# A mixer block's opening in written order: query tiles in two pairs, context statistics and first spectrum between the blocks of the first value head

## The chip, the cores and the metric

The kernel runs on one core of a Trainium2 chip. The metric is the device time of one launch in microseconds, the median of the runs shown; smaller is better. A core has five engines, each with its own queue of instructions: TensorE (PE, matrix products), VectorE (DVE), ScalarE (ACT), GpSimd (POOL, here mostly stores) and SyncE (SP, here all loads). An engine waits for another, or for a transfer, on semaphores.

## The reference

One layer of a backbone: two token mixers beside each other on the same normalised input (an mLSTM and a Hyena long convolution), a gated merge, and a feed-forward part. 512 latent tokens and 256 context tokens have 1024 features. What the opening computes of it:

```python
silu_c = jax.nn.silu(c);  silu_cc = jax.nn.silu(c_ctx)
mod  = silu_c  @ w_ada + b_ada          # shift sh1, scale sc1, ...
modc = silu_cc @ w_ada + b_ada
hc = rmsnorm(ctx, norm1_g) * (1.0 + csc1) + csh1
h  = rmsnorm(x,   norm1_g) * (1.0 + sc1)  + sh1
q  = h @ w_in[:, query columns] + b_in
vh = h (and hc) @ w_in[:, value columns] + b_in
g  = h (and hc) @ w_in[:, 16 gate columns] + b_in
# Hyena filters, for two orders and 1024 channels
a = sin(fr * (z @ w1 + b1)); a = sin(fr * (a @ w2 + b2)); a = sin(fr * (a @ w3 + b3))
k = (a @ w4) * window;  spectrum = rfft(two-sided k)
```

## The kernel before

Activations lie feature by feature: eight tiles of 128 features by 512 latent tokens, and eight of 128 by 256 context tokens. Every large product is made of three: each operand is split into a high part (rounded to the matrix format, `act.activation` with Copy) and a low part (the rest, `dve.tensor_sub`), and high by high, high by low and low by high are added in one PSUM bank (`mm3`, lines 233 to 235; in `v_head` lines 659 to 661).

The opening, in the order of the program's text:

- **Loads** (lines 261 to 1087, all on SyncE's queue): a table of vectors, the gate bias, the filter network's weights (`net`), the input `xT` in four pieces, constant matrices, the first half of the adaLN weights (sixteen pieces of 256 KB, `ada_load`) with the first query weights among them, then the first spectrum's decay row, skip and weights, three query weights, the Fourier table, the second adaLN half, and the context `cxT`. Each query weight is 512 KB, each of the four pieces of `xT` as well; `net` has 386 KB, the vectors 190, the constants 320, the gate bias 8, decay 256, skip 1, spectrum weights 256, the Fourier table 640, the context 1024.
- **Statistics** of the latent tokens: squares on ScalarE, sums on VectorE (`sq_sums`, lines 395 to 406), a product with ones, the reciprocal root (`rms_bcast`: scaling on VectorE at line 389, a power on GpSimd at line 391, a broadcast product at line 393), and the multiplication of the tiles (L1063, L1124).
- **adaLN** (`ada_first`, called for each half of the features): 32 products with the silu of both conditions in 32 rows (L337), a copy (L343), two transposes (L346), the additions of the bias (L353) and the scale vector (L354).
- **The filter network** (`filter_network`): three layers, each one product (L419, L422), six operations for the argument of the sine on VectorE (L425 to L430) and a sine on ScalarE (L432), then a split `stack`.
- **Modulation and the first four query tiles**: `modulate` makes high and low parts of the modulated tiles (L1094, L1099, L1100). `part(i, p)` adds for query tile i the products of feature half p. Half 0 needs the first adaLN half, half 1 the second.
- **The first spectrum** (`filter_spectrum`): eight products with the stack (L463, L464), then Fourier products (L233 to L235 on `dfh`, `dfl`).
- **Context**: statistics and eight tiles (L1150 the multiplication; `modulate` with `on_act`, where ScalarE makes both the high part, L1094, and the full value, L1097, and VectorE subtracts, L1100).
- **Value head 0** (`v_head`): six token blocks of 24 products, four latent and two of the context; each is followed by the bias on VectorE (L665), a store on GpSimd (L669) and the gate columns (L671). Then heads 1 to 3 with three larger blocks each, the other spectra between them, and the rest of the layer.

The order on each engine is not that of the text: a scheduler places instructions by their dependencies and priorities, and the text steers it in some places with `tc.issue_after(...)`, which lets what is inside come only after a given instruction, and with `tc.high_priority`. Loads wait for the buffers that they fill.

## Time and profile before

| | |
|---|---|
| median of 3 runs | 1218.85 us (1218.58 to 1222.32) |
| the profiled execution | 1219.83 us |
| its span, first to last instruction | 1218.0 us |
| TensorE busy | 1180.8 us, 97% |
| VectorE busy | 833.2 us, 68% |
| ScalarE busy | 528.9 us, 43% |
| GpSimd busy | 87.7 us, 7% |
| mean granted TensorE clock | 0.992 |

All views are of the one profiled execution, with times from the start of its span. A row of the timeline has the start in us, the duration in us, the engine, the line, the operation, the tile written and those read, the shape, the count of instructions merged into the row and, in brackets, how long the engine had sat idle before it and what ended that. PEclk is the share of full clock that TensorE was granted. `x4` on a row means four records; a product in plain float32 leaves two.

### The profile page before, as it was taken

The numbers are of one execution on the slowest core, as the hardware profiler recorded it, in microseconds if no ns is written. First come the engines' busy times: TensorE is split into PE (matmuls) and PEld (weight loads), VectorE is DVE, ScalarE is ACT, GpSimd is POOL, SyncE is SP. The second block draws the span as 40 slices with busy tenths as digits, with TensorE's granted clock in tenths as the row PEclk, the third lists the DMA queues.
The fourth block names the chain that finished last, engine by engine and source line by source line (L and its number), as shares of the span: only waits on it lengthen the run. The fifth ranks groups of instructions, "written<-read, shape, count | busy, mean of one in ns | idle before, by whom it ended". The sixth has DMA issues, their size and how long they took to land.

```text
span 1218.0 us, 16831 instructions
## 1 busy us (share of the span) xinstructions
PE 1180.8 (97%) x6440; PEld 1012.9 (83%) x6440; DVE 833.2 (68%) x1336; ACT 528.9 (43%) x824; POOL 87.7 (7%) x168
## 2 busy tenths in 40 slices
PE   4999999999999999999989999999999999999997
PEld 2799988888888888888778988889888888888886
DVE  5967797978989999897758896767753434432332
ACT  3754465753545444453655642333432232322221
POOL 0011110100010010101032031000000000000000
PEclk9999999999999999999989999999999999999998
DMA  9744453364244353434695686773443333233312
GB/s 346 248 159 163 136 185 106 133 237 143 75 162 137 130 174 102 147 106 155 211 319 180 196 265 218 260 234 121 140 138 104 90 100 101 85 95 96 96 48 70
DMA packets 63377, 189.04 MB, mean 155 GB/s; under 512 B 8760, under 2 KB 12608, under 8 KB 61120
## 3 DMA queue, kind: packets, MB, share of 16 engines
q1 hardware_dynamic: 51536, 150.20, 38.6%
q0 software_dynamic: 11760, 37.76, 8.7%
q8 instruction: 51, 0.84, 0.3%
q14 instruction: 30, 0.25, 0.1%
HBM read 154.37 MB, written 33.55 MB: 154 GB/s over the span
## 4 chain that ended last, share of the span: by engine, by line
PE 89%; DVE 4%; DMA 3%; ACT 2%; issue 1%; POOL 0%; SPq 0%; DVEq 0%; POOLq 0%; ACTq 0%
PE bank L233 26%; PE bank L234 26%; PE bank L235 26%; PE bank L659 2%; PE bank L660 2%; PE bank L661 2%; DMA wr<-qd 1%; DMA wr<-in_wph 1%; PE bank L616 1%; PE bank L463 1%; DVE wl L215 1%; PE bank L464 1%; ACT wh L214 1%; DMA ul<-in_xT 1%; PE bank L337 0%
## 5 line engine op out<-in xcount | busy, mean ns | idle before, releaser
L233 PE MATMUL bank<-hTh,wh 128*128 128x512 f32 (+1 forms) x952 | 366.6, 387 | 2.9 <-ACT hTh L1094 2.0
L234 PE MATMUL bank<-hTl,wh 128*128 128x512 f32 (+1 forms) x952 | 366.1, 386 | 2.9 <-DVE hTl L1100 2.2
L235 PE MATMUL bank<-hTh,wl 128*128 128x512 f32 (+1 forms) x952 | 365.6, 385 | 0.0
L214 ACT ACTIVATE wh<-wr 128x1024 fp32r<-128x1024 f32 (+1 forms) x167 | 172.2, 1033 | 400.8 <-PE bank L234 205.1
L215 DVE TENSOR_TENSOR wl<-wr,wh 128x1024 fp32r<-128x1024 f32 (+1 forms) x167 | 197.8, 1187 | 170.9 <-ACT wh L214 169.6
L233 PEld LDWEIGHTS bank<-hTh,wh 128*128 128x128 f32 x952 | 178.9, 188 | 37.5 <-ACT hTh L1094 2.2
L234 PEld LDWEIGHTS bank<-hTl,wh 128*128 128x128 f32 x952 | 179.0, 188 | 36.8 <-DVE hTl L1100 2.5
L235 PEld LDWEIGHTS bank<-hTh,wl 128*128 128x128 f32 x952 | 179.0, 188 | 34.6
L233 PE MATMUL bank<-big,wh 128*128 128x512 f32 (+1 forms) x266 | 94.7, 356 | 0.0
L234 PE MATMUL bank<-big,wh 128*128 128x512 f32 (+1 forms) x266 | 94.6, 356 | 0.0
L235 PE MATMUL bank<-big,wl 128*128 128x512 f32 (+1 forms) x266 | 94.6, 355 | 0.0
L372 DVE SCALAR_TENSOR_TENSOR wr<-wr,crow 128x1024 f32<-128x1024 f32 x32 | 38.9, 1218 | 28.3 <-DMA wr<-in_wada 28.2
L233 PEld LDWEIGHTS bank<-big,wh 128*128 128x128 f32 x266 | 50.3, 189 | 7.2
L235 PEld LDWEIGHTS bank<-big,wl 128*128 128x128 f32 x266 | 50.3, 189 | 7.1
L234 PEld LDWEIGHTS bank<-big,wh 128*128 128x128 f32 x266 | 50.3, 189 | 7.1
L214 ACT ACTIVATE hb<-hb 128x512 fp32r<-128x512 f32 (+1 forms) x49 | 36.5, 767 | 33.3 <-DVE hb L468 18.5
L1554 DVE TENSOR_TENSOR s<-s,bank 128x512 f32<-128x512 f32 x22 | 15.1, 686 | 46.4 <-PE bank L235 46.4
L391 POOL TENSOR_TENSOR rr<-rv,negh 128x2 f32<-128x2 f32 (+1 forms) x6 | 5.5, 924 | 510.7 <-DVE rv L389 510.7
L215 DVE TENSOR_TENSOR hb<-hb,hb 128x512 fp32r<-128x512 f32 (+1 forms) x49 | 40.4, 858 | 2.0 <-ACT hb L214 1.8
L659 PE MATMUL bank<-wh,hTh 128*128 128x256 f32 (+1 forms) x128 | 36.4, 285 | 0.0
L661 PE MATMUL bank<-wh,hTl 128*128 128x256 f32 (+1 forms) x128 | 36.4, 285 | 0.0
L660 PE MATMUL bank<-wl,hTh 128*128 128x256 f32 (+1 forms) x128 | 36.4, 284 | 0.0
(383 smaller groups left out, 2208.2 us busy)
## 6 DMA issues: line engine op xcount, KB each, us to landing
wr<-in_win SPq DMA_DIRECT2D x64, 512.0 KB, 3.8
wr<-in_w SPq DMA_DIRECT2D x60, 512.0 KB, 3.5
wr<-in_wada SPq DMA_DIRECT2D x32, 512.0 KB, 4.1
Kd<-K POOLq DMA_DIRECT2D x8, 1024.0 KB, 4.7
K<-Kd SPq DMA_DIRECT2D x8, 1024.0 KB, 6.4
wr<-in_wv SPq DMA_DIRECT2D x8, 512.0 KB
gmd<-s POOLq DMA_DIRECT2D x16, 256.0 KB, 2.5
wr<-in_wph SPq DMA_DIRECT2D x8, 512.0 KB, 4.2
```

The lines of the kernel that those rows point to most:

```text
L214: act.activation(hi, x, AF.Copy)
L215: dve.tensor_sub(lo, x, hi.bitcast(F32))
L233: pe.matmul(o, wh, xh, start=first, stop=False)
L234: pe.matmul(o, wh, xl, start=False, stop=False)
L235: return pe.matmul(o, wl, xh, start=False, stop=last)
L372: dve.scalar_tensor_tensor(w, w, 1.0, crow[:], op0=ALU.mult, op1=ALU.mult, accum_out=s)
L463: pe.matmul(ps[:], lhs, w4h, start=True, stop=False)
L464: pe.matmul(ps[:], lhs, w4l, start=False, stop=True)
L659: pe.matmul(o, xh, wh, start=bool(k == 0), stop=False)
L660: pe.matmul(o, xh, wl, start=False, stop=False)
L661: m = pe.matmul(o, xl, wh, start=False, stop=bool(k == KT - 1))
L1554: dve.tensor_tensor(t[:], t[:], pb[:], op=ALU.mult)
```

## The change

The opening is written as two blocks under a new context manager `in_order`, which makes every instruction of an engine depend on the one before it in the text. So inside, each engine runs what the text says, in the text's order. What the text now says:

- `xT` is loaded first, then vectors and constants, the first adaLN half, four query weights, `net`, the second adaLN half, the context, and last the first spectrum's tables. The gate bias comes with the value weights.
- The query weights are split in halves of four features (`early_hi`, `early_lo`), two of the first modulated tiles get their high part on VectorE (`hi_dve`), and `early_q` adds products by kind: for each tile first the high parts with both weights, later the low parts. Pieces of the second adaLN half and the first two layers of the filter network stand between them.
- The second half of the features is done for query tiles 0 and 1, then 2 and 3.
- `v_head` now yields after the products and after the bias of each block. Between the blocks of head 0 stand the end of the context statistics, the third network layer, the context tiles one after the other, the stack, the first spectrum's products, and the Fourier table's split.
- Behind that, head 1 may start on VectorE and ScalarE only after the fifth context tile (`marked`).

```diff
+    @contextmanager
+    def in_order():
+        traced = nc.cur_bb.bb.instructions
+        n, last, ends = len(traced), {}, []
+        yield ends
+        for i in traced[n:]:
+            if i.engine in last:
+                tc.add_manual_dep(
+                    i, last[i.engine], mybir.DependencyInfo(mybir.DependencyClass.NoSync, mybir.DependencyReason.DATA), reason="in_order"
+                )
+            last[i.engine] = i.name
+        ends.extend(i for i in traced[n:] if i.name in last.values())
...
+    def modulate(x, hi, lo, k, i, hi_dve=False, on_act=False):
+        a_, b_ = amod[:, k, i : i + 1], modT[:, 0, k, i : i + 1]
+        if hi_dve:
+            dve.tensor_scalar(hi, x, a_, b_, op0=ALU.mult, op1=ALU.add)
+        else:
+            act.activation(hi, x, AF.Identity, bias=b_, scale=a_)
+        yield
+        if on_act:
+            t = x
+            act.activation(t, x, AF.Identity, bias=b_, scale=a_)
...
+        dve.tensor_sub(lo, t, hi.bitcast(F32))
+        yield
...
+    def early_q(i, ks, w, x):
+        for k in ks:
+            count[i] += 1
+            m = pe.matmul(qps[i][:], early[i][w][:, k], hT[x][k][:], start=count[i] == 1, stop=count[i] == 3 * KT)
...
+    with in_order() as ends:
+        for q in range(4):
+            t = T(PH, [128, 2, SEQ], F32, ("uh", "ul")[q % 2])
+            dma(t[:], I["xT"][:, 2 * q : 2 * q + 2])
...
+            if q == 2:
+                dma(vecs[:], I["vecs"])
+        dma(mats[:], I["mats"])
...
+        units = [ada_load(PH, 0, slots[0])]
+        for i in range(NQ):
+            dma(raws[i], I["win"][FT_Q + i])
+        dma(net[:, :772], I["net"])
+        units.append(ada_load(PH, 1, slots[1]))
...
+        early_q(1, KA, 0, 1)
+        ahead(4)
+        early_q(2, KA, 0, 1)
+        early_q(3, KA, 0, 1)
...
-    with tc.issue_after(high), tc.issue_after(low):
-        part(0, 1)
-        csums, cb_ = bank(), bank()
-        for k in range(KT):
-            sq_sums(ac_, cxt[k], k, 2, PH, "s2", csums)
-        next(sp0)
-        part(1, 1)
-        rms_bcast(csums[:, :2], 2, cb_, PH, "s2")
-        part(2, 1)
-        for k in range(KT):
-            dve.tensor_tensor(cxt[k], cxt[k], cb_[:, :CTX], op=ALU.mult)
-        part(3, 1)
-        list(sp0)
...
-    for k in range(KT):
-        modulate(cxt[k], hcT[0][k], hcT[1][k], k, 1, True)
...
+    with in_order():
...
+        next(v0)
+        sq_sums(ac_, cxt[KT - 1], KT - 1, 2, PH, "s2", csums)
+        next(network)
+        next(v0)
+        next(v0)
+        rms_bcast(csums[:, :2], 2, cb_, PH, "s2")
+        for k in range(KT):
+            dve.tensor_tensor(cxt[k], cxt[k], cb_[:, :CTX], op=ALU.mult)
+            for _ in modulate(cxt[k], hcT[0][k], hcT[1][k], k, 1, on_act=True):
+                pass
+            if k == 4:
+                marked = list(nc.cur_bb.bb.instructions)
+                next(v0)
+                next(v0)
+        next(v0)
+        next(v0)
         stack = next(network)
+        next(v0)
         act.activation(dec[:], dec[:], AF.Abs)
         w4s = T(PH, [128, 2, 512], F32R, "hb")
         split(w4s[:, 0], w4s[:, 1], w4r)
...
+        open_spectrum = [spectrum(*sp.pop(0), (dec, skip, (w4s[:, 0], w4s[:, 1])))]
+        next(v0)
+        next(open_spectrum[0])
         split(fh[:], fl[:], fr)
...
+        list(v0)
+        next(open_spectrum[0])
+    opened.close()
+    for e in {i.engine for i in marked if i.engine in (nc.vector.engine, nc.scalar.engine)}:
+        opened.enter_context(tc.issue_after([i for i in marked if i.engine == e][-1]))
```

Three places show how the rows stand on the engines (the written order of the built program; a number behind a name is that of a buffer).

The first is SyncE's queue from the last pieces of the first adaLN half (into `K`) to the first piece of the second (into `hTh`). Before (`fd` is the decay row, `hb` the spectrum's weights and the Fourier table, `wr` the query weights):

```order
L325 DMA wr_144<-in_win 128x1024
L328 DMA K_157<-in_wada 128x512 x4
L448 DMA fd_293<-in_hdec 128x512
L450 DMA fs_295<-in_hskip 1x256
L1081 DMA hb_143<-in_hw 128x512
L1083 DMA wr_145<-in_win 128x1024
L1083 DMA wr_146<-in_win 128x1024
L1083 DMA wr_147<-in_win 128x1024
L1084 DMA hb_143<-in_dftf 128x1280
L328 DMA hTh_158<-in_wada 128x512
```

Now (`hb` from `in_net` is the filter network):

```order
L339 DMA K_129<-in_wada 128x512 x4
L339 DMA K_130<-in_wada 128x512 x4
L1108 DMA wr_117<-in_win 128x1024
L1108 DMA wr_118<-in_win 128x1024
L1108 DMA wr_119<-in_win 128x1024
L1108 DMA wr_120<-in_win 128x1024
L1109 DMA hb_103<-in_net 128x772
L339 DMA hTh_131<-in_wada 128x512
```

The spectrum's loads have moved behind the second adaLN half; the query weights and `net` stand ahead of it.

The second is VectorE at the end of the context statistics: `rv` is the scaling ahead of the power on GpSimd. Before, with the split of the value weights around it:

```order
L403 TENSOR_TENSOR s_39_133<-s_39_133,s_149_553 128x256
L215 TENSOR_TENSOR wl_697<-wr_695,wh_696 128x1088
L389 TENSOR_SCALAR rv_577<-bank_532 128x2
L215 TENSOR_TENSOR wl_704<-wr_702,wh_703 128x1088
L215 TENSOR_TENSOR wl_892<-wr_890,wh_891 128x512
L1150 TENSOR_TENSOR K_318<-K_318,bank_533 128x256
```

Now, where `hb_347` is the argument of the third network layer's sine and `bank_571` holds value block 0:

```order
L414 TENSOR_TENSOR s_69_193<-s_69_193,s_149_596 128x256
L436 TENSOR_SCALAR hb_347<-bank_602,hb_103 128x512
L437 TENSOR_SCALAR hb_347<-hb_347 128x512
L438 TENSOR_SCALAR hb_347<-hb_347 128x512
L439 SCALAR_TENSOR_TENSOR hb_347<-hb_347 128x512
L440 SCALAR_TENSOR_TENSOR hb_347<-hb_347 128x512
L441 TENSOR_SCALAR hb_347<-hb_347 128x512
L679 TENSOR_TENSOR s_151_611<-bank_571,s_131_506 128x256
L685 TENSOR_TENSOR gates_85<-bank_571,bgb_86 128x16
L400 TENSOR_SCALAR rv_640<-bank_522 128x2
```

The network layer and the block's two additions have come in front of the scaling. On TensorE there now stand, from the end of block 0 (`bank_571`) over block 1 (`bank_615`) to the start of block 2:

```order
L674 MATMUL bank_571<-wh_516,hTl_458 128x272
L417 MATMUL bank_522<-mats_70,s_69_193 128x1 x2
L433 MATMUL bank_602<-hb_347,hb_103 128x256 x2
L672 MATMUL bank_615<-wh_509,hTh_291 128x272
...
L674 MATMUL bank_615<-wh_516,hTl_458 128x272
L404 MATMUL bank_523<-mats_70,rr_642 128x128 x2
L672 MATMUL bank_670<-wh_509,hTh_291 128x272
```

The sums (L417) and the third layer (L433) follow block 0, and the broadcast (L404) follows block 1.

The third is VectorE and ScalarE in the context tiles (`K` is the context, `hb` its high and low parts). Before, on VectorE:

```order
L1150 TENSOR_TENSOR K_318<-K_318,bank_533 128x256
L215 TENSOR_TENSOR wl_929<-wr_927,wh_928 128x1024
L1150 TENSOR_TENSOR K_318<-K_318,bank_533 128x256 x7
L502 TENSOR_TENSOR hb_657<-bank_617,hb_657 128x512
L1100 TENSOR_TENSOR hb_668<-K_318,hb_667 128x256
L503 TENSOR_TENSOR hb_657<-bank_617,hb_657 128x512
L1100 TENSOR_TENSOR hb_668<-K_318,hb_667 128x256
```

And on ScalarE, with copies of the spectrum (L500, L501) between:

```order
L1094 ACTIVATE hb_667<-K_318,modT_78,amod_94 128x256
L1097 ACTIVATE K_318<-K_318,modT_78,amod_94 128x256
L500 ACTIVATE hb_657<-bank_619 128x512
L1094 ACTIVATE hb_667<-K_318,modT_78,amod_94 128x256 x2
L501 ACTIVATE hb_657<-bank_620 128x512
L1097 ACTIVATE K_318<-K_318,modT_78,amod_94 128x256 x2
L1094 ACTIVATE hb_667<-K_318,modT_78,amod_94 128x256 x2
```

Now, on VectorE from the scaling on:

```order
L400 TENSOR_SCALAR rv_640<-bank_522 128x2
L1225 TENSOR_TENSOR K_181<-K_181,bank_523 128x256
L1058 TENSOR_TENSOR hb_570<-K_181,hb_569 128x256
L1225 TENSOR_TENSOR K_181<-K_181,bank_523 128x256
L1058 TENSOR_TENSOR hb_570<-K_181,hb_569 128x256
```

And on ScalarE from the last square on:

```order
L413 ACTIVATE s_149_596<-K_181 128x256
L443 ACTIVATE hb_347<-hb_347 128x256
L1050 ACTIVATE hb_569<-K_181,modT_75,amod_90 128x256
L1054 ACTIVATE K_181<-K_181,modT_75,amod_90 128x256
L1050 ACTIVATE hb_569<-K_181,modT_75,amod_90 128x256
L1054 ACTIVATE K_181<-K_181,modT_75,amod_90 128x256
```

The multiplications, which stood together, now alternate with the subtractions, and on ScalarE each tile's two passes now follow each other directly.

More of the change, by code (lines that the diff above doesn't have):

```diff
@@ L1 @@
 import math
+from contextlib import contextmanager
 import numpy as np
@@ L260, in build @@
     vecs = T(P0, [128, nvec], F32, "vecs")
-    dma(vecs[:], I["vecs"])
     vec, at = {}, 0
@@ L1027, in spectrum @@
         return filter_spectrum(PH, PH, stack, negt, (fh, fl), o, c, loaded or spectrum_load(PH, o, c))
-    xt, cxt = [], []
-    network = filter_network(PH, net)
-    next(network)
-    xt, cxt = [], []
-    sums = bank()
-    ax_, ac_ = T(PH, [128, 512], F32, "s2"), T(PH, [128, 512], F32, "s2")
-    for q in range(4):
-        t = T(PH, [128, 2, SEQ], F32, ("uh", "ul")[q % 2])
-        dma(t[:], I["xT"][:, 2 * q : 2 * q + 2])
-        for j in range(2):
-            xt.append(t[:, j])
-    dma(mats[:], I["mats"])
@@ new lines, in modulated, with early_hi @@
+    def modulated(k, hi_dve=False):
+        for i, t in enumerate(("hTh", "hTl")):
+            hT[i].append(T(PT, [128, SEQ], F32R, t))
+        return modulate(xt[k], hT[0][k][:], hT[1][k][:], k, 0, hi_dve)
+    early, count = [], [0] * NQ
+    def early_hi(i, ks):
+        if len(early) <= i:
+            early.append([v[:, :1024].rearrange("p (a b) -> p a b", a=KT) for v in (T(PW, [128, WMAX], F32R, t, 4) for t in ("wh", "wl"))])
+        act.activation(early[i][0][:, ks], raws[i][:, ks], AF.Copy)
@@ L1075, in build @@
-    e0 = early_split(0)
-    with tc.issue_after(next(e0)):
-        tr, am, copy = ahead(8 - AH[0] - AH[1])
-    with tc.issue_after(am):
-        list(e0)
-    dec, skip = spectrum_vectors(PH, *sp[0])
-    dma(w4r, I["hw4"][sp[0]].rearrange("p f n -> p (f n)"))
-    for i in range(1, NQ):
-        dma(raws[i][:, :1024].rearrange("p (a b) -> p a b", a=KT), I["win"][FT_Q + i])
-    dma(fr, I["dftf"])
-    units.append(ada_load(PH, 1, slots[1]))
-    t = T(PH, [128, KT, CTX], F32, "K")
-    dma(t[:], I["cxT"])
@@ L1102, in modulated @@
-    def modulated(p):
-        for k in range(4 * p, 4 * p + 4):
-            for i, t in enumerate(("hTh", "hTl")):
-                hT[i].append(T(PT, [128, SEQ], F32R, t))
-            low = modulate(xt[k], hT[0][k][:], hT[1][k][:], k, 0, XA[p])
-        return low
-    def part(i, p):
-        gemm(qps[i], *early[i], *hT, SEQ, range(4 * p, 4 * p + 4))
-        if p:
-            act.activation(qb[i], qps[i][:], AF.Identity, bias=bin_[:, FT_Q + i : FT_Q + i + 1])
-    high, low = modulated(0)
```

219 lines of the change are left out of this document (134 added, 85 removed).

## The prediction

> **What bounds the kernel now.** I read the page first: its span and, in the 40 slices of 30 us, the busy tenths of TensorE (PE).
>
> ```profile
> span 1218.0 us, 16831 instructions
> PE   4999999999999999999989999999999999999997
> ```
>
> TensorE is busy in every slice but the first. So what the opening is late is not made up later, and the kernel costs the time at which TensorE's unbroken work begins plus that work. The second view, TensorE's instructions in order of time (start, duration, idle before and its releaser), shows that place and the ends of the stages that the change touches.
>
> ```profile
> 29.90 0.49 PE L233 MATMUL bank<-hTh,wh 128*128 128x512 f32 x1 [2.00 <-ACT hTh L1094]
> 32.61 0.80 PE L234 MATMUL bank<-hTl,wh 128*128 128x512 f32 x1 [2.22 <-DVE hTl L1100]
> 47.33 0.39 PE L337 MATMUL bank<-cx,silc 128*32 128x256 f32 x2
> 50.74 1.07 PE L233 MATMUL bank<-hTh,wh 128*128 128x512 f32 x4
> 67.14 0.29 PE L659 MATMUL bank<-wh,hTh 128*128 128x272 f32 x1
> 79.25 0.29 PE L659 MATMUL bank<-wh,hb 128*128 128x272 f32 x1
> 85.26 0.39 PE L463 MATMUL bank<-wh,astack 128*128 128x512 f32 x1
> ```
>
> Unbroken work begins at 32.61. By 50.74 the first-half products of the four query tiles, the spectrum's first products and the second adaLN half are done, and the second query half begins. Value head 0 runs in six blocks from 67.14 to 85.26, so a block costs 18.12 / 6 = 3.02 us; its context blocks begin at 79.25. One 128x512 product costs (1.07 - 0.39) / 3 = 0.227 us at full clock. From 50.74 to 85.26, 34.5 us, TensorE does not wait. I compare the change at the point where head 0 and the first spectrum are done: 85.26 now.
>
> **Step 1: the second query half starts earlier.** Third view: stretches of 10 us (the last two columns are DMA share and GB/s), the queue of SyncE, and the transfer times of the page's DMA part.
>
> ```profile
> 20.00:30.00 10.00, 7.44 (x75) 4.13 (x67) 8.76 (x21) 2.83 (x5) 0.00 (x0) 1.00 1.04 401
> 30.00:40.00 10.00, 7.78 (x27) 6.12 (x28) 9.94 (x17) 9.93 (x14) 0.00 (x0) 0.83 1.04 386
> 0.74 0.41 SPq L261 DMA_DIRECT2D vecs<-in_vecs  x1
> 2.14 0.43 SPq L1037 DMA_DIRECT2D uh<-in_xT  x1
> 37.19 1.00 SPq L328 DMA_DIRECT2D cx<-in_wada  x2
> cx<-in_wada SPq DMA_DIRECT2D x2, 256.0 KB, 5.4
> ```
>
> The DMA engines are saturated at about 390 GB/s. The last piece of adaLN's second half is issued at 37.19 + 1.00 - 0.33 = 37.86 and lands 5.4 us later, at 43.3. By the sizes of the tiles, 14,345 KB are queued up to it; the new queue puts 13,184 KB there (the decay row, skip, spectrum weights, Fourier table and gate bias, 1,161 KB, now come behind). 1.19 MB at 0.39 MB/us is 3.0 us. The first large load is issued at 0.74 instead of 2.14; of these 1.4 us, part was filled by the small loads, and I take half, 0.7 us (ends: 0 and 1.4). So the data are there at 39.6.
>
> The rows for what follows adaLN's last product (47.33):
>
> ```profile
> 47.78 0.38 ACT L343 ACTIVATE s<-bank 128x256 f32<-128x256 f32 x1 [5.07 <-PE bank L337]
> 49.27 0.17 DVE L354 SCALAR_TENSOR_TENSOR amod<-modT,vecs 128x8 f32<-128x8 f32 x1
> 49.47 1.52 ACT L1094 ACTIVATE hTh<-uh,modT,amod 128x512 fp32r<-128x512 f32 x2 [1.30 <-DVE amod L354]
> ```
>
> The last adaLN products take 0.7 us, copy 0.45, transposes 0.5; then eight query products are queued, 8 x 0.227 = 1.8 us, which hide VectorE's modulation vectors and the first modulated tile. 39.6 + 3.4 = **43.0** against 50.74. TensorE's own work before that just fits: the first query product, today at 29.90, comes 0.7 + 2.4 us earlier (908 KB less in front of adaLN's first half), at 26.8; 48 query products 10.9, adaLN 3.6, two network layers 1.0 and transposes 0.4 make 42.7. A half clock at its start, as today, would then cost up to 1.5 us, which I keep for the range. Splitting weights in halves adds some 0.06 us per extra instruction on ScalarE and VectorE; it lies under the wait for adaLN, and if that cover were gone it would cost below 1 us. The loads moved back on SyncE's queue land after the second adaLN half at the same rate: context 2.7 us later, the spectrum's 1,153 KB by 45.3, the value weights 2.8 us after that. They are needed at 52 (squares), 85 (spectrum) and 53.9 (block 0, 10.9 us after 43.0), and cost nothing there but for the 0.5 us in step 3.
>
> **Step 2: work that moves behind that point.** The third network layer and the spectrum's eight products, done before 50.74 today, now come later.
>
> ```profile
> 23.05 1.13 PE L422 MATMUL bank<-hb,hb 128*128 128x256 f32 x4
> 24.41 0.81 DVE L425 TENSOR_SCALAR hb<-bank,hb 128x512 f32<-128x512 f32 x1
> 25.13 0.68 DVE L1063 TENSOR_TENSOR ul<-ul,bank 128x512 f32<-128x512 f32 x1
> 28.09 0.43 DVE L430 TENSOR_SCALAR hb<-hb 128x512 f32<-128x512 f32 x1
> ```
>
> That is 1.06 + 8 x 0.23 = 2.9 us. With no new wait the compared point would come at 43.0 + 34.5 + 2.9 = 80.4: 4.9 us earlier.
>
> **Step 3: three new waits.** All come from the written order, which makes each engine take its instructions as listed. That VectorE does not pass a waiting instruction is seen here:
>
> ```profile
> 73.93 0.42 DVE L665 TENSOR_TENSOR s<-bank,s 128x256 f32<-128x256 f32 x1
> 74.78 0.43 DVE L1100 TENSOR_TENSOR hb<-K,hb 128x256 fp32r<-128x256 f32 x1 [0.43 <-ACT K L1097]
> 75.12 0.17 DVE L671 TENSOR_TENSOR gates<-bank,bgb 128x16 f32<-128x16 f32 x1
> ```
>
> The addition of L671 reads the bank that L665 had read at 73.93, yet it ran behind the subtraction that waited for ScalarE.
>
> *a) Context statistics.* After block 0, TensorE runs the sums (0.5), network layer 3 (1.0) and block 1 (3.0), then the broadcast product, which needs the reciprocal root. But VectorE has the six sine-argument operations in front (24.41 to 28.52 less 0.46 for the L1063 between them, 3.65 us), then block 0's two additions (0.4), then the scaling; GpSimd has a store issue in front of the power.
>
> ```profile
> 59.75 0.47 PE L406 MATMUL bank<-mats,s 128*128 128x1 f32 x3
> 60.93 0.70 POOL L391 TENSOR_TENSOR rr<-rv,negh 128x2 f32<-128x2 f32 x1 [41.44 <-DVE rv L389]
> 83.18 0.54 POOL L669 DMA_DIRECT2D vd<-s  x1 [2.47 <-DVE gates L671]
> 61.69 0.71 PE L393 MATMUL bank<-mats,rr 128*128 128x128 f32 x4
> ```
>
> From block 0's end: 1.5 + 0.15 + 3.65 + 0.4 + 0.15 + 0.2 + 0.54 + 0.70 = 7.3 us, while TensorE is free at 4.5: **2.8 us** idle. Behind the waiting broadcast stand blocks 2 and 3, ready but queued. Today layer 3 lies in the opening, and the scaling has no such chain in front.
>
> *b) The context tiles.*
>
> ```profile
> 62.88 0.41 DVE L1150 TENSOR_TENSOR K<-K,bank 128x256 f32<-128x256 f32 x1
> 65.14 2.40 DVE L1150 TENSOR_TENSOR K<-K,bank 128x256 f32<-128x256 f32 x7
> 65.03 0.59 ACT L1094 ACTIVATE hb<-K,modT,amod 128x256 fp32r<-128x256 f32 x1
> 65.66 0.60 ACT L1097 ACTIVATE K<-K,modT,amod 128x256 f32<-128x256 f32 x1
> ```
>
> Today VectorE multiplies seven tiles in a row (2.40 us) and ScalarE runs high and low passes in pairs, and from 62.88 to 79.25 TensorE has 16.4 us of other work. The new order goes tile by tile: multiply, two ScalarE passes (the second waits for the first: 0.63 + 0.60), subtract, and only then the next multiply. Per tile 0.41 + 0.04 + 0.63 + 0.60 + 0.04 + 0.33 = 2.05 us, eight tiles 16.4, plus 1.0 after the fifth for block 1's two additions (0.33 and 0.08 to the next, from 73.93) and one 512-wide subtraction (0.6, next to the 0.69 of row 35.53 below): 17.4 us. Behind each waiting subtraction stand only the next tile and weight halves of head 1, which TensorE needs after block 5. From the broadcast's start the last low tile is ready at 0.7 + 17.4 + 0.1 = 18.2, and block 4 ends 0.4 later, at 18.6. The work in front is the broadcast and blocks 2, 3 and 4: 0.7 + 9.06 = 9.7. **8.9 us** idle.
>
> *c) The spectrum behind it.* Sine, stack and weight split stand behind the eighth tile.
>
> ```profile
> 32.81 0.61 ACT L432 ACTIVATE hb<-hb 128x512 f32<-128x512 f32 x1
> 33.85 0.61 ACT L436 ACTIVATE astack<-hb 64x512 fp32r<-64x512 f32 x1
> 34.48 0.63 ACT L437 ACTIVATE s<-hb 64x512 fp32r<-64x512 f32 x1
> 35.53 0.69 DVE L438 TENSOR_TENSOR astack<-hb,s 64x512 fp32r<-64x512 f32 x1
> ```
>
> From the last ScalarE pass: 0.61 + 0.61 + 0.53 + 0.69 and the handovers give 2.5 for the stack, 2.9 with the split's high part, 3.7 with its low part behind block 3's additions; block 4 ends at 0.85. **2.5 us** idle in two pieces. I add 0.5 us for the sums in a), which may wait for value weights whose gate columns are issued late (nothing shows it: 0 to 1.5). Together 0.5 + 2.8 + 8.9 + 2.5 = 14.7 us: 80.4 + 14.7 = 95.1, **9.8 us later** than now.
>
> **Step 4: the clock.** How the granted clock (the third column from the right) takes a wait is shown by the kernel's longest later stall:
>
> ```profile
> 628.00:632.00 4.00, 1.59 (x4) 1.34 (x5) 4.00 (x7) 1.44 (x2) 3.33 (x7) 0.68 1.07 374
> 632.00:636.00 4.00, 4.00 (x12) 3.13 (x11) 3.08 (x8) 1.58 (x2) 1.46 (x3) 0.50 1.18 372
> 636.00:640.00 4.00, 4.00 (x34) 4.00 (x33) 4.00 (x7) 3.32 (x5) 0.00 (x0) 0.96 1.08 329
> ```
>
> Clock 0.68, then 0.50 with TensorE busy all 4 us, then 0.96. In b) TensorE works three short products of 0.38 us in each 2.05 us, so I expect half clock behind it; what it delays is only the busy part. I take 1.7 us (0 to 3.4): 3.4 us at half. The Trainium skill, page TensorE: Matmul & The Clock Gate, section Part 1: The HAM clock gate, says that for modeling the ramp is below 1% of a typical span and is not to be fitted; by that the sum would stay at 9.8 us (1228.7). 1% here is 12 us, so the rows decide.
>
> **Sum.** 9.8 + 1.7 = 11.5 us. The profiled execution took 1219.83 us, 1.0 above the median of 1218.85; 1231.3 against it is **1230.3** against the median.
>
> **Rivals.** *The lead is kept:* the waits of step 3 vanish under other work. It needs the idle of step 3 below 4.9 us; at none the time is 1218.85 - 4.9 = 1214. For it: the earlier start is real. Against it: the listed order has no TensorE work in those places. Chance 0.04. *The context tiles overlap as today:* ScalarE's 16 passes at 0.5 are 8 us, within the 9.7 of cover; then b) is 0, the sum -4.9 + 0.5 + 2.8 + 2.5 = +0.9: 1219.8. It needs VectorE to pass the waiting subtraction, against 74.78. Chance 0.06. *More than forecast:* a cold first stage (1.5), gate columns late (1.0) and two more half-clock windows (3.4) give +17.4: 1236.2 and above, chance 0.10. The forecast has 0.80.
>
> **Range.** Low: data 0.7 earlier, no 0.5, no clock cost, tiles 0.15 faster each (1.2): 11.5 - 4.1 = 7.4, with another 1 us for the hand-taken handovers, 1225. High: 1236.5. A measurement of this kernel can tell 0.3%, 3.7 us, from no change. Slower 0.90, same 0.06, faster 0.04.
>
> **What would show it.** In the changed profile: the second query half near 43; a wait of TensorE on GpSimd of about 2.8 us at the context broadcast; in block 4 gaps of 0.8 us alternating between ScalarE and VectorE over 10 us; 2 us before the spectrum's first product; a second stretch at half clock near 85. I am wrong if block 4 follows block 3 without gaps, or if the second query half starts after 46.

## The result, and the profile after

The changed kernel takes **1233.43 us** (median of 4 runs, 1232.34 to 1233.71) against 1218.9 us for the kernel before (4 runs): the ratio is 1.0114, with a 95% interval from 1.0102 to 1.0127. That is 14.5 us slower by the medians. The two profiled executions, 1233.58 and 1219.83 us, lie 13.75 us apart; the forecast for that difference was 11.5. Of all runs below, one slow execution of the last kernel (1426.45 us at a mean clock of 0.78) is left out of the medians and ratios.

The page of the changed kernel, span and busy tenths of TensorE in 40 slices (30.8 us each):

```profile
span 1231.8 us, 16843 instructions
PE   5969999999999999999989999999999999999997
```

Before, only the first slice stood out. Now the third does, from 61.6 to 92.4 us: 6 tenths. The first is fuller than before (5 instead of 4). The gain and the loss are both inside the opening, and the rest is as busy as it was.

TensorE's instructions in order of time in the changed kernel (start, duration, what, idle before and its releaser), at the places that the prediction named:

```profile
42.91 0.39 PE L1080 MATMUL bank<-hTh,wh 128*128 128x512 f32 x1
53.88 0.28 PE L672 MATMUL bank<-wh,hTh 128*128 128x272 f32 x1
58.23 0.61 PE L417 MATMUL bank<-mats,s 128*128 128x1 f32 x4 [1.16 <-DVE s L414]
58.69 1.11 PE L433 MATMUL bank<-hb,hb 128*128 128x256 f32 x4
59.45 0.47 PE L672 MATMUL bank<-wh,hTh 128*128 128x272 f32 x1
65.74 0.71 PE L404 MATMUL bank<-mats,rr 128*128 128x128 f32 x4 [2.91 <-POOL rr L402]
72.34 0.29 PE L672 MATMUL bank<-wh,hb 128*128 128x272 f32 x1
...
83.03 0.59 PE L672 MATMUL bank<-wh,hb 128*128 128x272 f32 x1 [0.37 <-ACT hb L1050]
84.12 0.59 PE L674 MATMUL bank<-wh,hb 128*128 128x272 f32 x1 [0.27 <-DVE hb L1058]
86.66 0.80 PE L474 MATMUL bank<-hb,astack 128*128 128x512 f32 x1 [1.94 <-DVE s L679]
90.53 0.43 PE L672 MATMUL bank<-wh,hb 128*128 128x272 f32 x1
94.19 0.28 PE L672 MATMUL bank<-wh,hTh 128*128 128x256 f32 x1
```

The second query half starts at 42.91 (50.74 before). Then come a wait of 1.16 us before the sums, layer 3 of the network (0.76 us, from 58.69 to 59.45), a wait of 2.91 before the context broadcast, block 4 from 72.34 to 84.71 (84.12 + 0.59; its 24 products need 3.2 us when nothing holds them up, as in the blocks before it), a wait of 1.94 before the spectrum (the row names L679, a value block's addition, which stands on VectorE right behind the subtraction L449 of the stack), and products of 0.63 and 0.43 us where 0.39 and 0.29 are usual. Head 0 ends at 94.19.

One piece of work must be added before this is compared with 85.26: the 36 transform products of the first spectrum. TensorE of the kernel before, their start and a place late in the trace:

```profile
62.93 0.28 PE L233 MATMUL bank<-hb,dfh 128*128 128x256 f32 x1
...
185.87 0.37 PE L756 MATMUL bank<-hb,mats 128*128 128x24 f32 x2 [0.52 <-DVE hb L755]
```

And of the changed kernel, the same two places:

```profile
99.10 0.64 PE L248 MATMUL bank<-hb,dfh 128*128 128x256 f32 x4
...
199.82 0.37 PE L771 MATMUL bank<-hb,mats 128*128 128x24 f32 x2 [0.52 <-DVE hb L770]
```

Before, the transforms run from 62.93 to 67.14, ahead of head 0; now they lie inside head 1, from 99.10 on. With their 4.2 us the changed kernel stands at 98.4 against 85.26, **13.1 us later**. Late in both traces, ahead of one and the same 24-column product, the difference is 199.82 - 185.87 = 13.95 us.

The lockstep of the context tiles, one tile on VectorE and ScalarE of the changed kernel:

```profile
66.49 0.42 DVE L1225 TENSOR_TENSOR K<-K,bank 128x256 f32<-128x256 f32 x1 [2.44 <-PE bank L404]
66.94 0.60 ACT L1050 ACTIVATE hb<-K,modT,amod 128x256 fp32r<-128x256 f32 x1 [9.20 <-DVE K L1225]
67.58 0.60 ACT L1054 ACTIVATE K<-K,modT,amod 128x256 f32<-128x256 f32 x1
68.22 0.43 DVE L1058 TENSOR_TENSOR hb<-K,hb 128x256 fp32r<-128x256 f32 x1 [1.31 <-ACT K L1054]
68.56 0.41 DVE L1225 TENSOR_TENSOR K<-K,bank 128x256 f32<-128x256 f32 x1
```

Multiply, high pass, second pass, subtract, and only then the next multiply: 68.56 - 66.49 = 2.07 us a tile (forecast 2.05). While VectorE waits for the second pass, ScalarE is at work; while VectorE subtracts and multiplies, ScalarE has nothing. From the start of the broadcast to the end of block 4 it is 84.71 - 65.74 = 19.0 us (forecast 18.6).

The granted clock in stretches of 10 us of the changed kernel (third column from the right):

```profile
60.00:70.00 10.00, 7.09 (x57) 6.87 (x56) 5.05 (x12) 2.16 (x4) 1.46 (x2) 1.00 0.04 15
70.00:80.00 10.00, 6.28 (x37) 4.88 (x36) 5.65 (x14) 6.52 (x11) 0.58 (x1) 0.92 0.13 33
80.00:90.00 10.00, 6.77 (x14) 4.31 (x15) 5.03 (x13) 8.69 (x14) 1.08 (x2) 0.50 0.30 111
90.00:100.00 10.00, 10.00 (x75) 9.81 (x75) 9.76 (x14) 5.86 (x7) 1.07 (x2) 0.90 0.41 139
```

Missing clock: (0.08 + 0.50 + 0.10) x 10 us at half speed make 13.6 us at half clock. In the kernel before the opening had 3.4 us of it (0.83 in its stretch from 30 to 40).

### The profile page after: what moved, and what is told of

Read it like the earlier page. It is cut to its first block, busy times and chain, and to the rows that moved or that the text cites. A ratio compares the mean times of both kernels' runs of the same rounds, so it can differ in the third digit from the quotient of the medians.

```text
span 1231.8 us, 16843 instructions
## 1 busy us (share of the span) xinstructions
PE 1189.3 (97%) x6440; PEld 1016.7 (83%) x6440; DVE 836.8 (68%) x1342; ACT 529.4 (43%) x826; POOL 87.9 (7%) x168
## 4 chain that ended last, share of the span: by engine, by line
PE 85%; DMA 6%; DVE 4%; ACT 3%; issue 1%; POOL 0%; SPq 0%; DVEq 0%; POOLq 0%; ACTq 0%
PE bank L248 26%; PE bank L249 25%; PE bank L250 25%; PE bank L673 2%; PE bank L674 1%; PE bank L672 1%; DMA wr<-in_wph 1%; DVE wl L230 1%; PE bank L474 1%; DMA wr<-in_wg 1%; PE bank L475 1%; ACT wh L229 1%; DMA hTh<-in_wada 1%; PE bank L627 1%; DMA K<-in_cxT 1%
## 5 line engine op out<-in xcount | busy, mean ns | idle before, releaser
L248 PE MATMUL bank<-hTh,wh 128*128 128x512 f32 (+1 forms) x920 | 353.8, 386 | 0.9 <-ACT hTh L1601 0.9
L249 PE MATMUL bank<-hTl,wh 128*128 128x512 f32 (+1 forms) x920 | 352.8, 385 | 0.6 <-DVE hTl L1602 0.6
L250 PE MATMUL bank<-hTh,wl 128*128 128x512 f32 (+1 forms) x920 | 352.6, 384 | 0.0
L248 PEld LDWEIGHTS bank<-hTh,wh 128*128 128x128 f32 x920 | 172.6, 188 | 33.6 <-ACT hTh L1601 1.3
L250 PEld LDWEIGHTS bank<-hTh,wl 128*128 128x128 f32 x920 | 172.6, 188 | 33.3
L249 PEld LDWEIGHTS bank<-hTl,wh 128*128 128x128 f32 x920 | 172.6, 188 | 33.2 <-DVE hTl L1602 0.8
```

The lines of the kernel that those rows point to most:

```text
L248: pe.matmul(o, wh, xh, start=first, stop=False)
L249: pe.matmul(o, wh, xl, start=False, stop=False)
L250: return pe.matmul(o, wl, xh, start=False, stop=last)
```

## The experiments

**Theory.** The loss comes from the order in which the second block (query half, head 0, context statistics, tiles, spectrum) is written, through the terms a), b), c) of the prediction and the half clock behind them. The rivals: late data, work that takes its time in any order, the clock alone.

### Context tiles in pairs

```
-for k in range(KT):
-    dve.tensor_tensor(cxt[k], cxt[k], cb_[:, :CTX], op=ALU.mult)
-    for _ in modulate(cxt[k], hcT[0][k], hcT[1][k], k, 1, on_act=True):
-        pass
+for k in range(KT):
+    dve.tensor_tensor(cxt[k], cxt[k], cb_[:, :CTX], op=ALU.mult)
+ms = [modulate(cxt[k], hcT[0][k], hcT[1][k], k, 1, on_act=True) for k in range(KT)]
+for k in range(0, KT, 2):
+    for m in (ms[k], ms[k + 1]) * 2:
+        next(m)
     if k == 4:
```

> Context tiles no longer one by one: all eight multiplications first, then the two ScalarE passes and the subtraction in pairs of tiles; nothing else is moved. Theory (the written order of the context tiles costs 9.2 us of waiting in block 4, 12.2 us from 72.34 to 84.56 where a block takes 3.0, and the half clock behind it another 2.7): block 4 takes about 5 us, the spectrum's first product starts near 79 instead of 86.66, no granted clock of 0.5 there, time about 1223 us (1221 to 1226). Rival, late data (the loads queued behind the second adaLN half set the place, not the order): block 4 still ends near 84 and the time stays at 1233. Rival, clock alone (the waits are as before, only the half clock goes): about 1230.7.

Measured: 1226.39 us, ratio to before 1.0053 (1.0035 to 1.0072): 7.0 us of the 14.5 are gone, not the 10.4 expected, and the time lies just outside the range. TensorE in this run:

```profile
66.44 0.38 PE L404 MATMUL bank<-mats,rr 128*128 128x128 f32 x1 [2.92 <-POOL rr L402]
73.04 0.29 PE L672 MATMUL bank<-wh,hb 128*128 128x272 f32 x1
...
77.61 0.39 PE L674 MATMUL bank<-wh,hb 128*128 128x272 f32 x1
80.14 0.80 PE L474 MATMUL bank<-hb,astack 128*128 128x512 f32 x1 [2.14 <-DVE s L679]
```

And its stretch behind that:

```profile
80.00:90.00 10.00, 9.86 (x51) 8.75 (x52) 8.33 (x13) 7.60 (x11) 0.54 (x1) 0.72 0.22 54
```

Block 4 takes 77.61 + 0.39 - 73.04 = 5.0 us as expected, so late data are ruled out as what sets block 4: it ends 6.7 us earlier (78.00 instead of 84.71) with the same loads. But the wait before the spectrum is 2.14 us, and the clock falls anyway (0.72 from 80 to 90), so the part of the forecast that counted on a full clock failed.

### Only the multiplications ahead

```
+for k in range(KT):
+    dve.tensor_tensor(cxt[k], cxt[k], cb_[:, :CTX], op=ALU.mult)
 for k in range(KT):
-    dve.tensor_tensor(cxt[k], cxt[k], cb_[:, :CTX], op=ALU.mult)
     for _ in modulate(cxt[k], hcT[0][k], hcT[1][k], k, 1, on_act=True):
```

> The changed kernel with the eight multiplications of the context tiles listed ahead of the loop, the two passes and the subtraction still tile by tile. It parts the two halves of the run with pairs. Theory: what makes the lockstep is VectorE's next multiplication behind the waiting subtraction, which leaves ScalarE idle 0.83 us a tile, 6.6 us over eight; the pairing adds only the 0.1 us by which a pass that does not wait for the one before is shorter in pace, 1.6 us. So block 4 ends near 79 (84.56 in the changed kernel, 77.85 with pairs) and the time is about 1227.8 us (1226.5 to 1229). Rival, the pairing is what counts: 1231 or more.

Measured: 1228.59 us, 1.0085 (1.0068 to 1.0101).

```profile
66.24 0.58 PE L404 MATMUL bank<-mats,rr 128*128 128x128 f32 x1 [2.92 <-POOL rr L402]
...
79.07 0.39 PE L674 MATMUL bank<-wh,hb 128*128 128x272 f32 x1 [0.49 <-DVE hb L1058]
```

From the broadcast to the end of block 4: 13.2 us (79.07 + 0.39 - 66.24), against 19.0 in the changed kernel and 78.00 - 66.44 = 11.6 with pairs. That would be 5.8 us for the multiplication behind the waiting subtraction (forecast 6.6) and 1.6 for the lack of pairing (forecast 1.6). But the clock is mixed into it: here the broadcast ran at half clock. VectorE's multiplications in this run, and then with pairs:

```profile
67.51 2.74 DVE L1225 TENSOR_TENSOR K<-K,bank 128x256 f32<-128x256 f32 x8 [2.96 <-PE bank L404]
```

```profile
67.18 2.74 DVE L1225 TENSOR_TENSOR K<-K,bank 128x256 f32<-128x256 f32 x8 [2.45 <-PE bank L404]
```

They start 1.27 us after the broadcast here, 0.74 with pairs and 0.75 in the changed kernel. Without that half microsecond the two parts are **6.3 and 1.1 us**. Both halves of the mechanism are there, the first near its forecast, the second smaller.

### Network layer 3 earlier

```
             for k in KB:
                 ...
+            if i == 0:
+                next(network)
             for j in (2 * i, 2 * i + 1):
                 early_q(j, KB, 0, 1)
...
         sq_sums(ac_, cxt[KT - 1], KT - 1, 2, PH, "s2", csums)
-        next(network)
         next(v0)
```

> The third network layer with its six sine-argument operations moves from behind block 0 to the middle of the second query half of tiles 0 and 1; nothing else is moved. Theory: TensorE's wait of 2.91 us on GpSimd before the context broadcast goes, and most of the 1.16 us before the sums; the chain of context tiles starts 3.8 us earlier and keeps its length, so all of it reaches the end: about 1229.6 us (1229 to 1231). Rival, the sine arguments only wait elsewhere (ahead of the low halves of the value weights, so that block 0 starts late): 1232 to 1233.5. Rival, the gain is taken up by a longer wait in block 4: 1233.

Measured: 1230.22 us, 1.0089 (1.0070 to 1.0108). The broadcast now follows block 1 without a wait (in the row there is none):

```profile
62.10 0.49 PE L404 MATMUL bank<-mats,rr 128*128 128x128 f32 x3
```

The wait on GpSimd is gone; the wait before the sums fell only from 1.16 to 0.67, less than expected. Together that is 3.4 us of waiting, and 3.2 came through by the medians. The reason for a) was right: six operations of VectorE stood in front of the scaling.

### The spectrum's stack ahead of the tiles

```
         rms_bcast(csums[:, :2], 2, cb_, PH, "s2")
+        stack = next(network)
+        act.activation(dec[:], dec[:], AF.Abs)
+        w4s = T(PH, [128, 2, 512], F32R, "hb")
+        split(w4s[:, 0], w4s[:, 1], w4r)
         for k in range(KT):
```

(and the same four lines removed behind the loop)

> The changed kernel with only the spectrum's sine, stack, absolute decay and weight split moved ahead of the context tiles, into the 9 us in which ScalarE has nothing (57.7 to 66.9). Theory: the wait of 1.94 us before the spectrum's first product goes; VectorE's two subtractions for it delay the first context tile by up to 0.4; block 4 and the half clock behind it stay: about 1231.9 us (1231.3 to 1232.5). Rival, the wait was hidden behind the tiles anyway or the tiles start later by as much: 1233.4.

Measured: 1232.09 us, 1.0101 (1.0076 to 1.0126): 1.3 us by the medians; the interval alone would not tell it from the changed kernel. The trace does: the spectrum's first product follows block 4 at once. (In the profiled execution the second query half began 0.7 us later, at 43.61, so a comparison of the two profiles alone would hide part of the gain.)

```profile
85.79 0.59 PE L674 MATMUL bank<-wh,hb 128*128 128x272 f32 x1 [0.27 <-DVE hb L1058]
86.18 0.63 PE L474 MATMUL bank<-hb,astack 128*128 128x512 f32 x1
```

### The clock by itself

Three runs put products that nothing reads into TensorE's waits, so that the order of all other instructions stays, and with it what they wait for on the other engines. The edit of the first; `spare` puts five products into a spare bank in block 4 of head 0:

```
                     pe.matmul(o, xh, wl, start=False, stop=False)
+                    spare(h, b)
                     m = pe.matmul(o, xl, wh, start=False, stop=bool(k == KT - 1))
+                    spare(h, b)
```

> Adds 80 products of 272 columns in block 4, five behind each place where TensorE waits for a context tile, into a spare bank that nothing reads; the order of all other instructions stays. Theory: the block's length is set by ScalarE and VectorE, so it stays near 12.2 us, but the granted clock stays at 1.0, and the spectrum's eight products take 1.9 us instead of 3.87 and block 5 3.0 instead of 3.66: 2.7 us less, about 1230.7 us (1230 to 1232). Rival, the half clock itself stretches block 4: the block shrinks too and the time falls by 5 us or more, to 1228. Rival, the half clock costs nothing that reaches the end: 1233.4.

> As the run with the spare products, with three instead of five behind each place where TensorE waits for a context tile (48 in all, their result is read by nothing). With five, TensorE's own work filled block 4 (13 products of 0.126 us a tile, 13.1 us for the block) and ate part of the gain. Theory (four windows at half clock cost 2.1 to 2.7 us behind block 4, nothing in it): with three the block keeps the 12.2 us of the changed kernel, the granted clock stays at 1.0, and the time is about 1231 us (1230.3 to 1231.8). Rival, TensorE at some 55% busy does not hold the clock: 0.5 again behind block 4, 1233.4.

> The clock by itself, once more: spare products of 272 columns, read by nothing, fill most of each wait of TensorE in the changed kernel: 7 before the sums (wait 1.16 us), 20 before the context broadcast (2.91), 4 behind each place of block 4 where it waits for a tile, 14 before the spectrum's first product (1.94), at 0.126 us each. All other instructions keep their order, so all waits for ScalarE, VectorE and GpSimd stay. Theory: granted clock 1.0 from 43 to 95, the spectrum's first product still near 86.7, head 1 starting at about 91.5 instead of 94.19: 2.7 us less, 1230.7 us (1230 to 1231.5). Rival, the half clock's loss is hidden behind the table loads and VectorE's work of the spectrum: 1233.4.

Measured: 1232.29 us with five, 1.0112 (1.0087 to 1.0138); 1234.05 with three, 1.0112 (1.0089 to 1.0134); 1232.22 with all waits filled, 1.0108 (1.0091 to 1.0125). By time, none can be told from the changed kernel (1.0114): by the medians 1.1, -0.6 and 1.2 us came instead of 2.7, and the intervals leave both nothing and nearly all of it open. The traces say more. With all waits filled, the stretch around the spectrum:

```profile
80.00:90.00 10.00, 9.08 (x54) 7.32 (x53) 4.87 (x13) 8.19 (x14) 1.08 (x2) 1.00 0.38 133
```

and TensorE there, the spectrum's first product and head 1's first:

```profile
87.47 0.50 PE L474 MATMUL bank<-hb,astack 128*128 128x512 f32 x1 [0.40 <-DVE s L689]
...
92.92 0.28 PE L680 MATMUL bank<-wh,hTh 128*128 128x256 f32 x1
```

The clock stayed at 1.00, and from the spectrum's first product to head 1 it took 92.92 - 87.47 = 5.45 us, against 94.19 - 86.66 = 7.53 in the changed kernel; with five it took 92.72 - 87.25 = 5.47. So the clock costs **2.1 us** there. In block 4 it costs almost nothing: from the start of the broadcast to the block's end it is 85.32 - 66.53 = 18.8 us at full clock against 19.0. Of the 2.7 that I had put down to it, 0.6 belongs to the spectrum's own work, which takes 5.45 instead of 1.85 + 3.02 = 4.87 at full clock too. In that execution the second query half also began 0.66 us later (43.57), which ate a third of the gain; head 1 starts 1.27 us earlier than in the changed kernel, and the two profiled executions differ by 0.80, so another half microsecond is lost behind that point, unexplained. With three products the half clock went elsewhere, in stretches of 4 us:

```profile
64.00:68.00 4.00, 2.41 (x11) 2.41 (x12) 0.42 (x1) 0.66 (x2) 1.46 (x2) 0.60 0.09 33
68.00:72.00 4.00, 4.00 (x20) 4.00 (x20) 1.51 (x4) 2.32 (x4) 0.00 (x0) 0.54 0.02 4
...
84.00:88.00 4.00, 1.81 (x9) 1.04 (x8) 2.68 (x7) 3.91 (x6) 1.08 (x2) 1.00 0.09 33
88.00:92.00 4.00, 4.00 (x16) 3.49 (x16) 2.92 (x5) 3.99 (x6) 0.00 (x0) 0.59 0.11 39
```

It came behind the wait of 2.92 us before the broadcast and again behind the spectrum's wait. That wait, of 2.91 us, had left the clock at 1.00 in the changed kernel's own profile.

### The new queue of loads in the kernel before

```
-    dec, skip = spectrum_vectors(PH, *sp[0])
-    dma(w4r, I["hw4"][sp[0]].rearrange("p f n -> p (f n)"))
     for i in range(1, NQ):
         dma(raws[i][:, :1024].rearrange("p (a b) -> p a b", a=KT), I["win"][FT_Q + i])
-    dma(fr, I["dftf"])
     units.append(ada_load(PH, 1, slots[1]))
+    dec, skip = spectrum_vectors(PH, *sp[0])
+    dma(w4r, I["hw4"][sp[0]].rearrange("p f n -> p (f n)"))
+    dma(fr, I["dftf"])
```

> The kernel before, with only its queue of loads changed: query weights 1 to 3 and the second adaLN half ahead of the spectrum's vectors, weights and Fourier table (1,153 KB), as in the change. Theory (step 1: the second query half waits for the landing of that adaLN half): it starts near 48 instead of 50.74, and the time falls by about 2.5 us, to 1216.4 (1215.5 to 1217.5). Rival, the spectrum's first products stand ahead of it on TensorE and now wait for their weights: 1219 or more.

Measured: 1224.75 us, 1.0039 (1.0029 to 1.0050): slower, and my expectation was wrong in sign. VectorE, ScalarE and TensorE of this run:

```profile
46.37 2.48 DVE L465 TENSOR_TENSOR hb<-bank,hb 128x512 f32<-128x512 f32 x4 [3.31 <-PE bank L464]
51.50 1.47 DVE L215 TENSOR_TENSOR dfl<-hb,dfh 128x1280 fp32r<-128x1280 f32 x1
52.90 0.35 DVE L353 TENSOR_TENSOR modT<-bank,vecs 128x4 f32<-128x4 f32 x4
53.49 1.52 ACT L1094 ACTIVATE hTh<-uh,modT,amod 128x512 fp32r<-128x512 f32 x2 [2.26 <-DVE amod L354]
54.35 2.08 PE L233 MATMUL bank<-hTh,wh 128*128 128x512 f32 x4 [2.64 <-ACT hTh L1094]
```

The last pieces of the adaLN half are issued earlier (34.33 instead of 37.19), but the spectrum's tables land later, and the spectrum's work on VectorE, from 46.37 to 52.97, now stands ahead of the modulation vectors (L353 at 52.90). TensorE's adaLN products of that half start at 47.11 (44.06 before), behind all first-half products and the spectrum's eight. The second query half starts at 54.35, and at half clock: its first four products take 2.08 us (1.07 before), the mean from 50 to 60 is 0.66. The rival had the place right, the spectrum in front. But on TensorE its products did not wait for their weights; the queue that counts is VectorE's. So the new order of loads gives no lead in the kernel before as its scheduler then orders it; the changed kernel, which has its lead, also lists the spectrum behind the query half.

### The second block without its written order

```
-    with in_order():
+    if True:
         for i in (0, 1):
             if i:
                 csums, cb_ = bank(), bank()
```

> The changed kernel with the written order kept in the opening but not in the second block (query half, head 0, context statistics and tiles, first spectrum): there the scheduler sets each engine's order again. Theory (the waits of 15 us between 43 and 94 come from the listed order alone, not from data, loads or work): no wait of TensorE above 1 us from 43 to 90, granted clock 1.0, second query half still at 42.9, time 1216 us (1214 to 1219). Rival, the waits belong to the moved work itself (network layer 3 and the spectrum behind block 0 need their time in any order): 1225 or more.

Measured: **1217.43 us**, 0.9985 (0.9971 to 1.0000): 16 us less than the changed kernel, from one line. Its stretches from 60 to 80:

```profile
60.00:70.00 10.00, 10.00 (x82) 10.00 (x81) 8.33 (x22) 7.87 (x15) 1.12 (x2) 1.00 0.08 28
70.00:80.00 10.00, 10.00 (x74) 9.34 (x74) 8.83 (x18) 9.21 (x15) 1.61 (x3) 1.00 0.67 196
```

And its context tiles on VectorE and ScalarE:

```profile
62.01 1.74 DVE L1225 TENSOR_TENSOR K<-K,bank 128x256 f32<-128x256 f32 x5
...
62.67 1.08 ACT L1050 ACTIVATE hb<-K,modT,amod 128x256 fp32r<-128x256 f32 x2
63.65 1.08 ACT L1054 ACTIVATE K<-K,modT,amod 128x256 f32<-128x256 f32 x2
```

TensorE is busy all 10 us of each stretch at a clock of 1.00. The scheduler puts five multiplications in a row and the passes in pairs, as in the kernel before, and also places block 1's addition in front of them. The moved work (network layer 3 and the spectrum's products) still takes its time on TensorE, but it needs no wait: the waits came from the listed order.

### The terms together

The edits of the pairs, of layer 3 and of the stack in one kernel, with the spectrum's eight products between blocks 3 and 4; then the same text without the written order of the second block.

> The three together, in written order still: network layer 3 in the second query half, sine, stack and weight split of the spectrum ahead of the context tiles, the tiles in pairs with all multiplications first, and the spectrum's eight products between blocks 3 and 4. Theory: none of the waits of the forecast's step 3 is left, the clock stays, and the lead of the opening is kept: second query half at 42.9, head 1 starting near 78, time about 1215 us (1213 to 1217), below the kernel before. Rival, the lead of the opening is no lead (something behind the second query half was always later, such as the value weights or the table loads): 1219 or more. Rival, the pairs of tiles still stall block 4 by 2 us or more: 1217 to 1219.

> The text of the run with the three changes together (network layer 3 early, spectrum's stack ahead of the tiles, tiles in pairs, spectrum before block 4), with the second block's order left to the scheduler. Theory: with the written order gone nothing is left to gain but the 0.6 us gap before the first transform product: 1215.5 us (1214 to 1217.5), as the two runs that each did one of these. Rival, the scheduler undoes what the text gains: above 1217.5.

Measured: 1216.6 us, 0.9982 (0.9969 to 0.9995), and **1216.46 us, 0.9969 (0.9957 to 0.9981)**. Of the forecast's waits, the first keeps only this one:

```profile
59.40 0.61 PE L417 MATMUL bank<-mats,s 128*128 128x1 f32 x4 [0.59 <-DVE s L414]
```

It keeps a written order too; so it is not the listing as such that costs, but this list. The second has the lowest ratio to its own runs of the kernel before, 3.1 parts in a thousand, 3.8 us of 1219; its interval overlaps those of the first and of the run without the written order, so the three are not told apart. About 5 us of lead at 80.4 were worked out; 2 to 4 reach the end. In the two profiled executions the second query half began late, at 43.82 and 44.74 instead of 42.91. In the last kernel two new gaps of 0.76 and 0.70 us stand ahead of the spectrum's transforms, near 86 and 89 us.

## Why the prediction was right

The direction and the mechanism held, and the time came 3.1 us above the forecast, inside the range. Term by term:

| term of the prediction | forecast, us | profile after, us | told apart by |
|---|---|---|---|
| step 1: second query half starts | 43.0 | 42.91 | 42.7 to 44.7 in the ten other runs with this opening |
| step 2: work moved behind | 2.9 | 0.8 (layer 3) + 1.85 = 2.6 | no wait of its own without the written order |
| step 3: the sums | 0.5 | 1.16 | 0.67 with layer 3 earlier; 1.14 to 1.87 in five other runs |
| a) context broadcast | 2.8 | 2.91 | gone with layer 3 earlier |
| b) context tiles | 8.9 | 12.4 - 3.2 = 9.2 | 6.3 + 1.1 for its two halves |
| c) spectrum | 2.5 | 1.94 | gone with the stack ahead |
| step 4: clock | 1.7 | 7.53 - 4.87 = 2.7 | 2.1 clock, 0.6 the spectrum's work |

By these, the compared point comes at 42.91 + 34.5 + 2.6 + 1.16 + 2.91 + 9.2 + 1.94 + 2.7 = 97.9; the trace has 98.4.

- **Step 1** came out to 0.1 us, in part by luck. The landing of the data fits: forecast at 39.6, and the last adaLN product starts at 39.9. But the check beside it, TensorE's own work up to that point, gave 42.7 from a first query product at 26.8 and 15.9 us behind it; the trace has 24.62 and 18.3. And in five of eleven profiled executions the half clock at the start came that the prediction kept for its range, at a price of 0.5 to 1.8 us. There is also a condition that the prediction did not state: in the kernel before, the new order of loads alone made this point later, not earlier.
- **Step 2** took layer 3 at 1.06 us, the distance to the next product in a row of the kernel before; it took 0.76.
- **Step 3, b)** is the largest term, and its rate of 2.05 us a tile was read off rows of the kernel before by adding up a chain that did not exist there. That works because every link had a row.
- **The sums** were taken at 0.5 of a range from 0 to 1.5 and cost 1.16: the squares stood on ScalarE behind the split of the value weights' second half, and that waited for its gate columns, as feared there:

```profile
52.22 1.11 ACT L229 ACTIVATE wh<-wr 128x1088 fp32r<-128x1088 f32 x1 [1.89 <-DMA wr<-in_wg]
53.24 0.40 ACT L410 ACTIVATE s<-K 128x256 f32<-128x256 f32 x1
```

- **c)** was forecast as 2.5 in two pieces. By its terms, the stack with the high half of the weights is 2.9 - 0.85 = 2.05, and 0.45 is left for their low half. The first came as 1.94. The second is hidden under the first product, which takes 0.80 at half clock; with the clock kept it showed as a gap of 0.23.
- **Step 4** was under-sized. I allowed 3.4 us at half clock; there were 13.6. Of these, 8.3 lie in block 4 and in the wait behind it, where ScalarE and VectorE set the pace and TensorE's speed hardly matters, and 5.3 behind 86.66, where TensorE's work is what counts. So the price is 2.1 us and not half of 13.6. The page TensorE: Matmul & The Clock Gate of the Trainium skill, section Part 1: The HAM clock gate, says that for modeling the penalty of the ramp is below 1% of a typical kernel span and that one should not fit to a specific cold count. The trace agrees on the size: 2.1 us of 1232 is 0.17%. It is still about a sixth of the 13.75 us by which the two kernels differ.
- **The signs** that the prediction named came: 42.91, a wait of 2.91 on GpSimd, 1.94 before the spectrum, half clock around 85. The gaps of block 4 alternate between ScalarE and VectorE as it said, but are 0.57 to 0.58 us at full clock and 0.27 to 0.37 at half clock, with one of 1.59, and not 0.8.
- **What is left open:** between 98 us and 200 us another 0.8 us gathers, without a gap. Some 600 products of 256 columns follow each other there at 0.120 us on average instead of 0.119, which is about that much. No run was made for it, and what slows them stays open. The spectrum's own 0.6 us of step 4 has 0.23 in the gap named under c); the rest is not told apart.

The rival in which the tiles overlap as today needed VectorE to pass the waiting subtraction. It does not: L1225 at 68.56 stands behind L1058 at 68.22, which waited 1.31 us. The kept lead of the first rival, 1214, is what the last two kernels approach.

## What to carry to other kernels

Where an order is written out by hand, go through each engine's list and ask at each instruction that waits what stands behind it; a tile-by-tile loop over two engines makes them take turns, and writing the same loop in stages (all of the first operation, then pairs) gave 7 us here for no work saved. Price a stall by what another engine sets in it: here a slow clock cost 0.2 us inside block 4, whose pace other engines set, and 2.1 us behind it. Before moving a load forward, ask whether something that now gets its data later stands ahead of the work that the move was to speed up.

## What the runs showed of the hardware that was not expected

- A wait of the same length at the same place took the clock in some executions and not in others: the 2.9 us before the broadcast left 1.00 from 60 to 70 in the changed kernel, with pairs and with five spare products, 0.83 there with the multiplications ahead and with the stack ahead, and 0.60 from 64 to 68 with three spare products.
- TensorE need not be idle in one piece to lose its clock: in block 4 no gap was above 1.59 us, TensorE counts as busy 6.28 and 6.77 of the 10 us in the two stretches from 70 to 90 (only 1.6 of the 4 us from 74 to 78, just ahead of the fall), and 13.6 us went by at half clock. With spare products in all waits (9.08 and more of each 10 us from 50 to 100 busy) it stayed at 1.00.
- The second query half began between 42.7 and 44.7 us in eleven profiled executions of one and the same opening. The granted clock early in it sorts them: where it was 1.00 from 20 to 30 us, as in the changed kernel, the half began between 42.70 and 42.91 (six executions); where it was 0.83, between 43.43 and 44.74 (five). The latest of these, the last kernel:

```profile
20.00:30.00 10.00, 8.15 (x49) 5.13 (x48) 8.00 (x18) 6.00 (x10) 0.00 (x0) 0.83 1.03 399
```

There the last adaLN products, those on `cx`, start between 41.1 and 41.7; in the changed kernel they start between 38.7 and 39.9, spread out, presumably as their pieces land. So where the clock was lost, TensorE's own work set the place and not the loads. A difference of a microsecond between two kernels in a single profile can be this alone.
